# A convolution's shifted copies by quarters of the channels, chunk statistics moved behind the last step, and a layer norm in another order, in a two-layer trunk on one core

## The chip, the cores and the metric

One Trainium2 chip, one of its cores. The metric is device time of one launch in microseconds (us), median of three runs, beside the time of a second kernel. PE is TensorE's matmuls, PEld its weight loads, DVE is VectorE, ACT is ScalarE, POOL is GpSimd, SP is SyncE, which here issues nearly all transfers.

## The reference, cut to what matters

A latent sequence of 256 tokens and a context of 256 tokens (512 columns together), 1024 channels, two layers. Only the mixer of the first layer is touched:

```python
def conv_module(h, w1, b1, dw, dw_b, norm_g, w2):
    y = h @ w1 + b1
    a, gt = jnp.split(y, 2, axis=-1)
    y = a * jax.nn.sigmoid(gt)
    y = lax.conv_general_dilated(y, dw[:, None, :], window_strides=(1,),
        padding=[(15, 15)], dimension_numbers=('NWC', 'WIO', 'NWC'),
        feature_group_count=D_MODEL) + dw_b          # 31 taps, each channel by itself
    y = jax.nn.silu(layer_norm(y, norm_g))           # mean and variance over the 1024 channels
    return y @ w2
```

Beside it each layer needs `silu(c) @ ada_w` for both conditions, from which shift, scale and gate of every sub-layer come. Float32 products are made on TensorE from split operands: an operand is the sum of a high part and a low part, and one product is three matmuls (high by high, low by high, high by low; lines 201 to 203, `mm3`).

## The kernel before, in words

The 1024 channels are eight chunks of 128 partitions; a chunk has 512 columns. Step `s` of the loop over chunks makes the gate half `g` and the value half `a` of chunk `s` (each 24 matmuls of 128x128 by 512), multiplies them into `y`, and meanwhile convolves the chunks before it. Of the 31 taps of a chunk, 16 run on TensorE, the rest on DVE (`lacc`, L557 and L559) and on POOL with ACT (`pacc`, L537 to L546).

TensorE needs four shifted copies of `y` on four groups of 32 partitions. They come by way of DRAM: `bounce_out` (L505) writes `y` to a scratch `yd` of 4 quarters x 32 channels, `bounce_in` (L508 to L517) loads the diagonal weights `dg` and then the tile `z4` (its transfers show as `z<-yd`). `dwconv_pe` (L526, name `cv`) contracts over 32 channels x 4 shifts, a quarter of the channels at a time. Chunk `s`'s copies are asked for in step `s` and used in step `s + 2`. SP issues transfers strictly in the order written, and an issue that waits holds up those behind it. There are two `z4` tiles.

The order is written out by hand: `pin` keeps an instruction in program order on its engine. Around the steps stand twenty blocks of the adaptive weights (`ada` 0 to 19): `begin` is eight matmuls (L240), `evict` a copy on ACT (`adasb`), `cols` two matmuls with that copy (L252), `finish` two small ACT operations (`mods`). They fill TensorE where it would wait.

The layer norm's sums are taken per chunk by `stats` (L588): two matmuls with a 1/1024 weight, on the chunk and on its square (`square`, L583, ACT, two tiles). Chunks 0 to 3 are summed inside steps 6 and 7, ahead of the taps' matmuls; 4 to 7 after the last step. Then `srow` (ACT copy), `stats_t` (L771, sums to columns), `mean_bc` (L774, mean to all partitions), `mb` (ACT), eight subtractions on POOL (L790), the inverse root on DVE (L806 to L815), `rstd_bc` (L799), and for every chunk `zt` (DVE, L829), `zs` (ACT, Silu, L838), high part `ah_z` and low part `al_z` (DVE, L325 and L326). The product with `w2` (tiles `w`) follows, in two halves of 512 output channels; its weights come as `w2_00`, `w2_01` (first half), `w2_10`, `w2_11` (second half), each split into `wh` on ACT and `wl` on DVE. Three tiles hold raw weights.

Of the kernel before, what the change touches and what calls it, by code (L numbers as in the profile page):

```python
# [64 lines left out]
ADA_AUX = (16, 17, 18, 19)
ADA_K4 = (8, 9, 18)
# [17 lines left out]
def trunk_kernel(ctx: ExitStack, tc, x_in, ctx_in, cond, small, consts, rope, dist, ada, adas, adat,  # L84
# [67 lines left out]
    def load(src, n=2048, name="w", also=lambda i: None):  # L152
        raw = wp.tile([P, 2048], F32, tag="raw", name="raw_" + name)
        also(nc.sync.dma_start(raw[:, :n], src))
        return raw
# [333 lines left out]
    def glu(ch, pa, sg):  # L489
# [9 lines left out]
            pin(nc.gpsimd.tensor_tensor(yv, yv, sg, op=ALU.mult))  # L499
        return y  # L500

    def bounce_out(ch, y):

# [1 line left out]
        pin(nc.sync.dma_start(yd.rearrange("q c t -> (q c) t"), y.rearrange("p s t -> p (s t)")))  # L505
        return yd

    def bounce_in(ch, yd):  # L508

# [4 lines left out]
        w = 2 * YW - 3
        for s in range(4):
            pin(nc.sync.dma_start(z4[32 * s:32 * s + 32, :, 0:w], yd[:, :, s:s + w].rearrange("q c t -> c q t")))
# [64 lines left out]
    def square(ch):  # L581
        sqs[ch] = cv.tile([P, 512], F32, tag="sq", name="sq", bufs=2)
        pin(nc.scalar.activation(sqs[ch], yc[:, ch, :], AF.Square))  # L583

    def stats(ch):
        for i, src in enumerate((yc[:, ch, :], sqs.pop(ch))):
            q = 2 * (ch % 2) + i
            pin(nc.tensor.matmul(pst[32 * q:32 * q + 32, :], mean32, src, start=(ch < 2), stop=(ch >= KC - 2)))  # L588
# [143 lines left out]
    fills = [pA.tile([P, 4096], F32, tag=tag, name=f"raw_fill_{tag}") for tag in ("ah", "al")]
    pin(nc.gpsimd.memset(fills[0][:, 0:1], 0.0))
    for i in range(12, 16):
        t = fills[(i - 12) // 2][:, 2048 * (i % 2):2048 * (i % 2) + 2048]
# [3 lines left out]
    for i in (16, 17):
        t = cv.tile([P, 4, 2 * YW], F32, tag="z4", name=f"raw_ada{i}", bufs=Z4).rearrange("p q t -> p (q t)")[:, 0:2048]  # L740
        pin(nc.sync.dma_start(t, ada[ADA_PE.index(i)]))
        ada_raws[i] = halves(t)
# [17 lines left out]
    cols(11)  # L760
    total(d)
    finish(11)
    square(d)
    stats(KC - 1)
    begin(12)
# [2 lines left out]
    evict(12)
    ptk = aux("stats_t")
    for t in range(4):  # L770
        pin(nc.tensor.matmul(ptk[:, 2 * t:2 * t + 2], srow[:, P * t:P * t + P], sel2, start=True, stop=True))  # L771
    pmd = aux("mean_bc")
    for q in range(4):
        pin(nc.tensor.matmul(pmd[32 * q:32 * q + 32, :], sel2[:, 0:1].to_broadcast([P, 32]), srow, start=True, stop=True))  # L774
    mb = cv.tile([P, 512], F32, tag="sq", name="mb", bufs=2)
    begin(13)
    cols(12)
    pin(nc.scalar.activation(mb, pmd, AF.Copy))
    evict(13)
    finish(12)  # L780
    cols(13)
    finish(13)
    gate_to_rows(0, 0, pin)
    gates = [gate_bc(0, 0, 0, pin), gate_bc(0, 0, 1, pin)]
# [1 line left out]
    ada_raws[19] = ada_load(19, pin)
    begin(14)
    evict(14)
    for ch in range(KC):
        pin(nc.gpsimd.tensor_tensor(yc[:, ch, :], yc[:, ch, :], mb, op=ALU.subtract))  # L790
    st = cv.tile([P, 4, 2], F32, name="st")
    nc.vector.tensor_copy(st.rearrange("p t i -> p (t i)"), ptk[:, 0:8])
    md, vv = st[:, :, 0], st[:, :, 1]
# [12 lines left out]
    nc.vector.tensor_tensor(mq, md, md, op=ALU.mult)  # L806
# [4 lines left out]
    nc.vector.tensor_scalar(nh, va, -0.5, None, op0=ALU.mult)
    for i in range(3):
        nc.vector.tensor_tensor(pt, nh, rn, op=ALU.mult)
        nc.vector.tensor_tensor(pt, pt, rn, op=ALU.mult)
        nc.vector.scalar_tensor_tensor(rn, pt, 1.5, rn, op0=ALU.add, op1=ALU.mult)  # L815
# [1 line left out]
    cols(14)
    finish(14)
    begin(15)
    evict(15)  # L820
    cols(15)
    finish(15)
# [11 lines left out]
    for ch in range(KC):  # L834
        if ch + 1 < KC:
            z_norm(ch + 1)
        zs = pz[ch % 2]
        pin(nc.scalar.activation(zs, zts[ch], AF.Silu, scale=cn[:, ch:ch + 1]))  # L838
        split_to(z[0][:, ch, :], z[1][:, ch, :], zs, pin)
        if ch == W2_AT:  # L840
            split_w2(0, 1, None, pin)
        if ch in (2, 4):
            begin(15 + ch // 2)
            evict(15 + ch // 2)
        if ch in (3, 5):
            cols(15 + ch // 2)
            finish(15 + ch // 2)
    cvs.close()
    pB = ctx.enter_context(tc.tile_pool(name="pB", bufs=1))
    for i in range(2):  # L850
# [28 lines left out]
        for _ in range(min(n, len(adr))):  # L879
            ada_next(adr.pop(0))  # L880

    for n in range(2):
# [4 lines left out]
        w = kview(w2p[n, 0] + w2p[n, 1], 512)
        order = ([(t, k) for k in range(KC) for t in range(4)] if n == 0
                 else [(t, k) for t in range(4) for k in range(KC)])
        for t, k in order:  # L890
# [5 lines left out]
            if not n and t == 3 and k in (3, 5):  # L896
                begin(18 + k // 5)
                evict(18 + k // 5)
            if not n and t == 3 and k in (4, 6):
                cols(18 + k // 6)  # L900
                finish(18 + k // 6)
# [568 lines left out]
```

## Time and profile before

| | |
|---|---|
| runs | 1097.85 us median, 1096.79 to 1098.8 |
| profiled execution | 1100.03 us, its span 1098.2 us |
| PE busy over the span | 1069.6 us (97%) |
| steps with the taps, 60.00 to 154.86 us | PE busy 92.41 of 94.86 us |
| last value half to first matmul with `w2`, 154.86 to 185.52 us | PE busy 27.04 of 30.66 us |
| from there to the next norm's first transposes, 185.52 to 232.01 us | PE busy 46.49 of 46.49 us |
| median landing of one `z<-yd` transfer of 284.5 KB | 5.2 us |

The span runs from the first to the last instruction; the execution's own time is 1.8 us more. In rows of a timeline or of the chain of waits the first number is the start, the second the duration. In rows of stretches each engine has its busy time and its instructions, and at the end stand TensorE's granted clock, the share of the 16 DMA engines, and GB/s.

### The profile page before, as it was taken

Reading aid. Unit: us, or ns where it says so; the run is one execution under the profiler, and the core shown is the slowest. Engines: PE = TensorE matmul, PEld = TensorE weight load, DVE = VectorE, ACT = ScalarE, POOL = GpSimd, SP = SyncE. Lnnn points to the kernel's source line nnn. Section 1 sums busy time; section 2 is a strip of 40 time slices with the busy share of each in tenths; the row PEclk is TensorE's granted clock in tenths of the full one; section 3 lists DMA queues with packets and bytes.
Section 4 is the critical chain, followed back from the end, with each engine's and each line's share of the span. In section 5 each row is a group of like instructions: output and inputs, shape, how many; then the busy total and the mean of one; then the engine's idle time right before and its main releaser. Section 6 shows DMA issues by size and latency. Waiting matters only on the chain.

```text
span 1098.2 us, 13530 instructions
## 1 busy us (share of the span) xinstructions
PE 1069.6 (97%) x5322; PEld 844.4 (77%) x5322; DVE 696.1 (63%) x1138; ACT 418.6 (38%) x610; POOL 161.7 (15%) x120
## 2 busy tenths in 40 slices
PE   7899998999999999999999999999999989999998
PEld 4566655788888888888888788888888868888886
DVE  4797874667999886636554786357454555555445
ACT  5473564344221222212231663324332453444442
POOL 0076863030000000000000430000000461000000
PEclk9999999999999999999999999999999999999999
DMA  9477778822576677433323342234233344455551
GB/s 367 183 191 224 221 211 330 346 94 81 203 252 230 230 272 255 163 115 115 115 75 118 139 157 93 111 134 163 106 115 115 115 159 159 167 186 192 192 182 49
DMA packets 35185, 190.16 MB, mean 173 GB/s; under 512 B 3953, under 2 KB 4657, under 8 KB 16049
## 3 DMA queue, kind: packets, MB, share of 16 engines
q1 hardware_dynamic: 34688, 188.01, 48.9%
q10 hardware_dynamic: 434, 1.29, 0.3%
q8 instruction: 42, 0.69, 0.3%
q14 instruction: 21, 0.17, 0.0%
HBM read 185.86 MB, written 3.42 MB: 172 GB/s over the span
## 4 chain that ended last, share of the span: by engine, by line
PE 88%; DVE 4%; ACT 3%; DMA 2%; issue 1%; POOL 1%; SPq 0%; ACTq 0%; POOLq 0%
PE u L203 4%; PE u L201 4%; PE fa L202 4%; PE u L202 4%; PE fa L203 4%; PE fb L202 4%; PE fa L201 4%; PE fb L203 4%; PE fb L201 4%; PE v L202 3%; PE v L203 3%; PE v L201 3%; PE dn L203 3%; PE dn L201 3%; PE dn L202 3%; PE g L201 2%
## 5 line engine op out<-in xcount | busy, mean ns | idle before, releaser
L172 DVE TENSOR_TENSOR wl_gu<-raw_gu,wh_gu 128x1024 fp32r<-128x1024 f32 x76 | 92.2, 1222 | 82.3 <-ACT wh_gu L164 81.5
L164 ACT ACTIVATE wh_gu<-raw_gu 128x1024 fp32r<-128x1024 f32 x84 | 88.0, 1058 | 139.3 <-PE fb L202 52.6
L870 DVE SCALAR_TENSOR_TENSOR junk<-raw_adat,crow 128x1024 f32<-128x1024 f32 x80 | 97.7, 1221 | 0.9
L172 DVE TENSOR_TENSOR wl_dn<-raw_dn,wh_dn 128x1024 fp32r<-128x1024 f32 x38 | 46.5, 1224 | 45.5 <-ACT wh_dn L164 45.2
L201 PE MATMUL fa<-ah_h0f,wh_gu 128*128 128x512 f32 (+1 forms) x192 | 72.0, 376 | 1.0 <-DVE ah_h0f L325 1.0
L202 PE MATMUL fa<-al_h0f,wh_gu 128*128 128x512 f32 (+1 forms) x192 | 72.2, 376 | 0.1
L201 PE MATMUL fb<-ah_h0f,wh_gu 128*128 128x512 f32 (+1 forms) x192 | 72.1, 376 | 0.0
L203 PE MATMUL fa<-ah_h0f,wl_gu 128*128 128x512 f32 (+1 forms) x192 | 72.0, 375 | 0.0
L202 PE MATMUL fb<-al_h0f,wh_gu 128*128 128x512 f32 (+1 forms) x192 | 72.0, 375 | 0.0
L203 PE MATMUL fb<-ah_h0f,wl_gu 128*128 128x512 f32 (+1 forms) x192 | 72.0, 375 | 0.0
L164 ACT ACTIVATE wh_dn<-raw_dn 128x1024 fp32r<-128x1024 f32 x38 | 40.3, 1060 | 80.3 <-PE dn L203 35.5
L201 PE MATMUL u<-wh_gu,ah_h1f 128*128 128x512 f32 x160 | 63.6, 397 | 0.0
L172 POOL TENSOR_TENSOR wl_qk<-raw_qk,wh_qk 128x1024 fp32r<-128x1024 f32 x4 | 9.6, 2397 | 362.6 <-DVE res L356 350.1
L202 PE MATMUL u<-wl_gu,ah_h1f 128*128 128x512 f32 x160 | 62.5, 392 | 0.0
L203 PE MATMUL u<-wh_gu,al_h1f 128*128 128x512 f32 x160 | 62.4, 391 | 0.0
L542 POOL TENSOR_TENSOR pacc<-pacc,pr 128x512 f32<-128x512 f32 x39 | 58.7, 1506 | 17.9 <-ACT pr L541 15.6
L559 DVE SCALAR_TENSOR_TENSOR lacc<-y,sm,lacc 128x512 f32<-128x512 f32 x65 | 49.1, 755 | 2.1
L202 PE MATMUL v<-wl_v,ah_h 128*128 128x512 f32 x128 | 50.4, 393 | 0.0
L203 PE MATMUL v<-wh_v,al_h 128*128 128x512 f32 x128 | 50.1, 391 | 0.0
L201 PE MATMUL dn<-wh_dn,ah_hid 128*128 128x512 f32 x128 | 49.9, 390 | 0.0
L202 PE MATMUL dn<-wl_dn,ah_hid 128*128 128x512 f32 x128 | 49.8, 389 | 0.0
L203 PE MATMUL dn<-wh_dn,al_hid 128*128 128x512 f32 x128 | 49.8, 389 | 0.0
(309 smaller groups left out, 2665.2 us busy)
## 6 DMA issues: line engine op xcount, KB each, us to landing
raw_gu<-in_gu_dram SPq DMA_DIRECT2D x44, 1024.0 KB, 4.8
raw_adat<-in_adat_dram SPq DMA_DIRECT2D x28, 1024.0 KB, 4.8
raw_dn<-in_dn_dram SPq DMA_DIRECT2D x19, 1024.0 KB, 4.7
raw_ada<-in_ada_dram SPq DMA_DIRECT2D x11, 1024.0 KB, 11.0
z<-yd SPq DMA_DIRECT2D x32, 284.5 KB, 5.2
raw_qk<-in_wqk_dram SPq DMA_DIRECT2D x8, 1024.0 KB, 4.7
raw_v<-in_wv_dram SPq DMA_DIRECT2D x8, 1024.0 KB, 4.8
raw_g<-in_wg_dram SPq DMA_DIRECT2D x8, 1024.0 KB, 4.8
```

Source lines behind the costliest of these rows:

```text
L164: also(nc.scalar.activation(hi[:, :m], raw[:, c:c + m], AF.Copy))
L172: also((eng or nc.vector).tensor_tensor(lo[:, :m], raw[:, c:c + m], hi[:, :m].bitcast(F32), op=ALU.subtract))
L201: also(nc.tensor.matmul(o, a[0], b[0], start=first, stop=False))
L202: also(nc.tensor.matmul(o, a[0], b[1], start=False, stop=False))
L203: also(nc.tensor.matmul(o, a[1], b[0], start=False, stop=last))
L542: pin(nc.gpsimd.tensor_tensor(pacc, pacc, pr, op=ALU.add))
L559: pin(nc.vector.scalar_tensor_tensor(cacc, a, w, cacc, op0=ALU.mult, op1=ALU.add))
L870: pin(nc.vector.scalar_tensor_tensor(junk, raw[:, c, :], 1.0, crow[:, s, :], op0=ALU.mult, op1=ALU.mult, accum_out=mods[l][:, c0 + c, s:s ...
```

## The change

- The four transfers that fill `z4` go by quarter of the channels and no longer by shift: each writes 128 partitions (32 channels x 4 shifts) of one quarter's columns, instead of 32 partitions (one shift) of all quarters. Bytes and number of transfers stay. Partitions are now ordered channel by shift, and the weights `dwd` are laid out to match.
- `dg` is asked for in `bounce_out`, ahead of `y`'s way out.
- Chunks 0 to 5 are squared and summed after the last step, between the blocks 8 to 11, chunk 6 after them. Chunk 7 has sums of its own: eight matmuls with one column straight into `stats_t`, added on DVE. The mean goes out by `token_row`, as the inverse root does.
- The inverse root stands ahead of block 13, most of its operands in PSUM.
- `ah_z` is written by a second ACT operation with Silu; DVE's cast is gone.
- Blocks 13 to 19 stand later, four of them within the first half of the `w2` product; the gates' transfers stand behind the load of `w2_10`. Blocks 14, 15 and 19 load into `z4` tiles, 12 and 13 into one freed tile instead of two, and 16 into small tiles.

```diff
@@ bounce_out, bounce_in
+        n = GROUPS[ch]
+        dgs[ch] = cv.tile([P, MAXG, 4, 32], F32, tag="dg", name="dg", bufs=2)
+        pin(nc.sync.dma_start(dgs[ch][:, :n], dwd[:, ch, :n]))
         yd = dr.tile([4, 32, 2 * YW], F32, name=f"yd{ch}")
...
-        for s in range(4):
-            pin(nc.sync.dma_start(z4[32 * s:32 * s + 32, :, 0:w], yd[:, :, s:s + w].rearrange("q c t -> c q t")))
-        return z4, dg
+        for q in range(4):
+            src = yd[q]
+            pin(nc.sync.dma_start(z4[:, q, 0:w], bass.AP(src.tensor, src.offset, [[2 * YW, 32], [1, 4], [1, w]])))
+        return z4, dgs.pop(ch)
@@ inside the steps
-        if step >= KC - 2:
-            stats(2 * (step - KC + 2))
-            stats(2 * (step - KC + 2) + 1)
...
-        if step >= KC - 3:
-            i = 2 * (step - KC + 3)
-            square(i)
-            square(i + 1)
+        if step == KC - 1:
+            square(0)
+            square(1)
@@ after the last step
     cols(8)
     finish(8)
     begin(9)
-    stats(4)
-    stats(5)
-    square(c)
+    stats(0)
+    stats(1)
+    square(2)
+    square(3)
     evict(9)
     begin(10)
     cols(9)
     finish(9)
+    stats(2)
+    stats(3)
+    square(4)
+    square(5)
     evict(10)
...
+    for i, src in enumerate((yc[:, d, :], sqs.pop(d))):
+        for t in range(4):
+            pin(nc.tensor.matmul(ptk[:, 16 + 2 * t + i:17 + 2 * t + i], src[:, P * t:P * t + P], mean32[:, 0:1],
+                                 start=True, stop=True))
+        if not i:
+            begin(12)
+    pin(nc.vector.tensor_tensor(st[:, 1, :], ptk[:, 16:24], st[:, 0, :], op=ALU.add))
...
+    pmd = token_row(md, "mean_bc")
@@ for every chunk of z
+        pin(nc.scalar.activation(z[0][:, ch, :], zts[ch], AF.Silu, scale=cn[:, ch:ch + 1]))
         pin(nc.scalar.activation(zs, zts[ch], AF.Silu, scale=cn[:, ch:ch + 1]))
-        split_to(z[0][:, ch, :], z[1][:, ch, :], zs, pin)
+        pin(nc.vector.tensor_tensor(z[1][:, ch, :], zs, z[0][:, ch, :].bitcast(F32), op=ALU.subtract))
         if ch == W2_AT:
             split_w2(0, 1, None, pin)
+        if ch == 0:
+            finish(13)
+            evict(14)
+            load_to(19, z4_tile(19))
+            w2r[1, 0] = load(w2[1, 0], name="w2_10", also=pin)
+        if ch == 1:
+            cols(14)
+            finish(14)
+            gate_to_rows(0, 0, pin)
+            gates = [gate_bc(0, 0, 0, pin), gate_bc(0, 0, 1, pin)]
...
+    w2r[1, 1] = load(w2[1, 1], name="w2_11", also=pin)
@@ first half of the w2 product
+        if t == 3 and k in W2_ADA:
+            i = 17 + W2_ADA.index(k)
+            if i > 17:
+                cols(i - 1)
+                finish(i - 1)
+            if i < 20:
+                begin(i)
+                evict(i)
```

The first place is SP's queue around chunk 1's copies (`yd1` is chunk 1 in DRAM). Before:

```order
L505 DMA yd1_586<-y_579 128x572 [waits DMAHW3_49,Pool_49]
L512 DMA dg_588<-in_dwd_dram 128x512
L516 DMA z4_590<-yd1_586 32x4x569 [waits DMAHW5_49,DMAHW3_49]
L516 DMA z4_590<-yd1_586 32x4x569 [waits DMAHW6_49]
L154 DMA raw_w1b5_698<-in_w1b_dram 128x2048 [waits DMAHW1_49,DVE_49]
```

The same place in the change:

```order
L509 DMA dg_586<-in_dwd_dram 128x512 [waits DMAHW3_49]
L511 DMA yd1_588<-y_579 128x572 [waits DMAHW4_49,Pool_49]
L520 DMA z4_590<-yd1_588 128x1x569 [waits DMAHW4_49]
L520 DMA z4_590<-yd1_588 128x1x569 [waits DMAHW6_49]
L155 DMA raw_w1b5_698<-in_w1b_dram 128x2048 [waits DMAHW1_49,DVE_49]
```

`dg` moved ahead of `yd1`, and each copy writes 128 partitions.

The second place is TensorE from the taps of the last chunk (`cv7`) to `rstd_bc`. Before:

```order
L526 MATMUL cv7_1490<-z4_1365,dg_1363 32x512 x15
L252 MATMUL ada11_1481<-cst_81,adasb_1507 128x2 [waits Activation_49]
L588 MATMUL stats_529<-yc_528,cst_81 32x512 [waits DVE_49]
L588 MATMUL stats_529<-sq_1515,cst_81 32x512 [waits Activation_49]
L240 MATMUL ada12_1519<-raw_fill_ah_1426,csil_113 32x256 x7
L771 MATMUL stats_t_1532<-cst_81,srow_1528 128x2 [waits Activation_49]
L774 MATMUL mean_bc_1537<-srow_1528,cst_81 32x512 [waits PE_49]
L240 MATMUL ada13_1543<-raw_fill_ah_1426,csil_113 32x256 x7
L252 MATMUL ada13_1543<-cst_81,adasb_1555 128x2 [waits Activation_49]
L287 MATMUL gr00_1563<-cst_81,gcs_1564 16x128 [waits PE_49,Activation_49]
L240 MATMUL ada14_1581<-raw_fill_al_1427,csil_113 32x256 x7
L799 MATMUL rstd_bc_1618<-cst_81,rn_1604 128x128 [waits DVE_49]
```

The same place in the change:

```order
L530 MATMUL cv7_1492<-z4_1349,dg_1345 32x512 x12
L792 MATMUL stats_t_1523<-cst_81,srow_1486 128x2 [waits Activation_49]
L797 MATMUL stats_t_1523<-cst_81,yc_528 128x1 [waits DVE_49]
L241 MATMUL ada12_1534<-raw_fill_1410,csil_113 32x256 x7
L797 MATMUL stats_t_1523<-cst_81,sq_1521 128x1 [waits Activation_49]
L785 MATMUL mean_bc_1551<-cst_81,st_1528 128x128 [waits DVE_49]
L241 MATMUL ada13_1580<-raw_fill_1410,csil_113 32x256 x7
L253 MATMUL ada12_1534<-cst_81,adasb_1549 128x2 [waits Activation_49]
L785 MATMUL rstd_bc_1593<-cst_81,rn_1566 128x128 [waits DVE_49,Activation_49]
```

The sums of chunks 0 to 6 stand ahead of `cv7` now, and one block less stands between `cv7` and `rstd_bc`.

The third place is ACT within the first half of the `w2` product, from the value of chunk 5 on. Before:

```order
L838 ACTIVATE zs1_1645<-zt_1691,sm_79 128x512 [waits DVE_49]
L259 ACTIVATE mods0_107<-ada17_1696,sm_79 128x2 [waits PE_49]
L838 ACTIVATE zs0_1644<-zt_1707,sm_79 128x512 [waits DVE_49]
L838 ACTIVATE zs1_1645<-zt_1716,sm_79 128x512 [waits DVE_49]
L164 ACTIVATE wh_w2_10_1883<-raw_w2_10_1728 128x1024 [waits DMAHW4_49]
```

The same place in the change:

```order
L845 ACTIVATE ah_z_1611<-zt_1684,sm_79 128x512 [waits DVE_49]
L846 ACTIVATE zs1_1614<-zt_1684,sm_79 128x512
L165 ACTIVATE wh_w2_10_1889<-raw_w2_10_1628 128x1024 [waits DMAHW1_49]
L260 ACTIVATE mods0_107<-ada16_1689,sm_79 128x2 [waits PE_49]
L845 ACTIVATE ah_z_1611<-zt_1700,sm_79 128x512 [waits DVE_49]
```

The split of `w2_10`, which waits for its load, moved ahead of the values of chunks 6 and 7.

More of the change, by code (lines that the diff above doesn't have):

```diff
@@ L63 @@
 W2_AT = 3
+W2_ADA = (3, 4, 5, 6)
 PACC = 2
[L65 to L66 removed]
+ADA_AUX = (14, 15, 16, 17, 18, 19)
+ADA_K4 = (8, 9, 16)
 T2 = 5
@@ L587, in stats @@
             q = 2 * (ch % 2) + i
-            pin(nc.tensor.matmul(pst[32 * q:32 * q + 32, :], mean32, src, start=(ch < 2), stop=(ch >= KC - 2)))
+            pin(nc.tensor.matmul(pst[32 * q:32 * q + 32, :], mean32, src, start=(ch < 2), stop=(ch >= KC - 3)))
     ys, zs4, cbs = {}, {}, {}
@@ L730, in trunk_kernel, with load_to, z4_tile @@
     dve_taps(d, cut, TAPS)
[L732 to L735, printed above, removed]
+    def load_to(i, t):
         pin(nc.sync.dma_start(t, ada[ADA_PE.index(i)]))
         ada_raws[i] = halves(t)
+    def z4_tile(i):
+        return cv.tile([P, 4, 2 * YW], F32, tag="z4", name=f"raw_ada{i}", bufs=Z4).rearrange("p q t -> p (q t)")[:, 0:2048]
+    fill = pA.tile([P, 4096], F32, tag="ah", name="raw_fill")
+    for i in (12, 13):
+        load_to(i, fill[:, 2048 * (i % 2):2048 * (i % 2) + 2048])
+    load_to(14, z4_tile(14))
     w2r[0, 1] = load(w2[0, 1], name="w2_01", also=pin)
[L739 to L742, printed above, removed]
     cols(8)
@@ L752, in trunk_kernel @@
     finish(9)
+    stats(2)
+    stats(3)
+    square(4)
+    square(5)
     evict(10)
-    stats(c)
+    begin(11)
     cols(10)
     finish(10)
-    begin(11)
-    cbs[d] = dwconv_pe(d, zs4.pop(d))
+    stats(4)
+    stats(5)
+    square(c)
     evict(11)
[L760 to L765, printed above, removed]
+    stats(c)
     srow = t2("srow")
     pin(nc.scalar.activation(srow, pst, AF.Copy))
[L768 to L784, printed above, removed]
-    ada_raws[18] = ada_load(18, pin)
[L786 to L793, printed above, removed]
+    cols(11)
+    finish(11)
+    cbs[d] = dwconv_pe(d, zs4.pop(d))
+    load_to(15, z4_tile(15))
+    ada_raws[16] = ada_load(16, pin)
+    ada_raws[17] = ada_load(17, pin)
+    ada_raws[18] = ada_load(18, pin)
+    total(d)
+    square(d)
     def token_row(cols, name):
@@ L816, in trunk_kernel @@
-    prs = token_row(rn, "rstd_bc")
[L817 to L822, printed above, removed]
+    ptk = aux("stats_t")
+    for t in range(4):
+        pin(nc.tensor.matmul(ptk[:, 2 * t:2 * t + 2], srow[:, P * t:P * t + P], sel2, start=True, stop=True))
+    st = cv.tile([P, 2, 8], F32, name="st")
+    pin(nc.vector.tensor_copy(st[:, 0, :], ptk[:, 0:8]))
+    for i, src in enumerate((yc[:, d, :], sqs.pop(d))):
+        for t in range(4):
+            pin(nc.tensor.matmul(ptk[:, 16 + 2 * t + i:17 + 2 * t + i], src[:, P * t:P * t + P], mean32[:, 0:1],
+                                 start=True, stop=True))
+        if not i:
+            begin(12)
@@ new lines, in trunk_kernel @@
+    pin(nc.vector.tensor_tensor(st[:, 1, :], ptk[:, 16:24], st[:, 0, :], op=ALU.add))
+    pin(nc.vector.tensor_tensor(ptk[:, 24:32], ptk[:, 16:24], st[:, 0, :], op=ALU.add))
+    md, vv = (st[:, 1, :].rearrange("p (t i) -> p t i", i=2)[:, :, i] for i in range(2))
+    mdp = ptk[:, 24:32].rearrange("p (t i) -> p t i", i=2)[:, :, 0]
+    evict(12)
+    pmd = token_row(md, "mean_bc")
+    mb = cv.tile([P, 512], F32, tag="sq", name="mb", bufs=2)
+    pin(nc.scalar.activation(mb, pmd, AF.Copy))
+    for ch in range(KC):
+        pin(nc.gpsimd.tensor_tensor(yc[:, ch, :], yc[:, ch, :], mb, op=ALU.subtract))
@@ new lines, in trunk_kernel @@
+    rn = cv.tile([P, 4], F32, name="rn")
+    mq, va, nh, pt = (ptk[:, c:c + 4] for c in (32, 36, 8, 12))
+    pin(nc.vector.tensor_tensor(mq, mdp, md, op=ALU.mult))
+    pin(nc.vector.scalar_tensor_tensor(va, vv, EPS, mq, op0=ALU.add, op1=ALU.subtract))
+    pin(nc.vector.tensor_scalar(rn.bitcast(I32), va.bitcast(I32), -0.5, 1597463007.0, op0=ALU.mult, op1=ALU.add))
+    pin(nc.vector.tensor_scalar(nh, va, -0.5, None, op0=ALU.mult))
+    for i in range(3):
+        pin(nc.vector.tensor_tensor(pt, nh, rn, op=ALU.mult))
+        pin(nc.vector.tensor_tensor(pt, pt, rn, op=ALU.mult))
+        pin(nc.vector.scalar_tensor_tensor(rn, pt, 1.5, rn, op0=ALU.add, op1=ALU.mult))
@@ L824, in trunk_kernel @@
+    begin(13)
+    cols(12)
+    evict(13)
+    prs = token_row(rn, "rstd_bc")
+    cols(13)
+    finish(12)
+    begin(14)
     z = new_act(pA, "z")
@@ L837, in trunk_kernel, with w2_order @@
         zs = pz[ch % 2]
+        pin(nc.scalar.activation(z[0][:, ch, :], zts[ch], AF.Silu, scale=cn[:, ch:ch + 1]))
         pin(nc.scalar.activation(zs, zts[ch], AF.Silu, scale=cn[:, ch:ch + 1]))
-        split_to(z[0][:, ch, :], z[1][:, ch, :], zs, pin)
+        pin(nc.vector.tensor_tensor(z[1][:, ch, :], zs, z[0][:, ch, :].bitcast(F32), op=ALU.subtract))
         if ch == W2_AT:
             split_w2(0, 1, None, pin)
+        if ch == 0:
[8 more added lines that the diff above has]
+            gates = [gate_bc(0, 0, 0, pin), gate_bc(0, 0, 1, pin)]
         if ch in (2, 4):
-            begin(15 + ch // 2)
-            evict(15 + ch // 2)
+            begin(14 + ch // 2)
+            evict(14 + ch // 2)
         if ch in (3, 5):
-            cols(15 + ch // 2)
-            finish(15 + ch // 2)
+            cols(14 + ch // 2)
+            finish(14 + ch // 2)
+    w2r[1, 1] = load(w2[1, 1], name="w2_11", also=pin)
+    def w2_order(n):
+        return ([(t, k) for k in range(KC) for t in range(4)] if n == 0
+                else [(t, k) for t in range(4) for k in range(KC)])
+    pw = [acc(f"w2_0{t}") for t in range(4)]
+    w = kview(w2p[0, 0] + w2p[0, 1], 512)
+    for t, k in w2_order(0):
+        tk = slice(P * t, P * t + P)
+        mm3(pw[t], (z[0][:, k, tk], z[1][:, k, tk]), w(k), k == 0, k == KC - 1)
+        if k == KC - 1:
+            residual(t, 0, pw[t], gates[t // 2])
+        if t == 3 and k in W2_ADA:
[6 more added lines that the diff above has]
+                evict(i)
     cvs.close()
     pB = ctx.enter_context(tc.tile_pool(name="pB", bufs=1))
-    for i in range(2):
-        w2r[1, i] = load(w2[1, i], name=f"w2_1{i}", also=pin)
     ads = ExitStack()
@@ L880, in fill_rows @@
             ada_next(adr.pop(0))
-    for n in range(2):
+    for n in (1,):
         pw = [acc(f"w2_{n}{t}") for t in range(4)]
-        if n:
-            split_w2(n, 0)
-            split_w2(n, 1)
+        split_w2(n, 0)
+        split_w2(n, 1)
         w = kview(w2p[n, 0] + w2p[n, 1], 512)
-        order = ([(t, k) for k in range(KC) for t in range(4)] if n == 0
-                 else [(t, k) for t in range(4) for k in range(KC)])
-        for t, k in order:
+        for t, k in w2_order(n):
             tk = slice(P * t, P * t + P)
@@ L895, in trunk_kernel @@
                 residual(t, n, pw[t], gates[t // 2], last)
[L896 to L901, printed above, removed]
             if n and (t, k) == (1, KC - 1):
```

18 lines of the change are left out of this document (3 added, 15 removed).

## The prediction

> **What bounds the kernel now.** I read the page's busy times first, then the stretches around the changed code, then TensorE's own waits, and last the transfers behind the longest wait.
>
> ```profile
> PE 1069.6 (97%) x5322; PEld 844.4 (77%) x5322; DVE 696.1 (63%) x1138; ACT 418.6 (38%) x610; POOL 161.7 (15%) x120
> ...
> 60.00:154.86 94.86, 92.41 (x498) 60.52 (x497) 76.74 (x87) 51.56 (x75) 69.85 (x56) 0.98 0.80 227
> 154.86:185.52 30.66, 27.04 (x282) 13.47 (x282) 15.46 (x33) 13.23 (x37) 15.03 (x13) 1.00 0.84 297
> 185.52:232.01 46.49, 46.49 (x244) 36.66 (x245) 33.17 (x59) 17.74 (x31) 1.29 (x2) 1.00 0.64 249
> ```
>
> TensorE is busy 97% of the span, so a change is worth what it takes from TensorE's idle time, from its slow stretches and from its list of work. In the changed code it idles 94.86 - 92.41 = 2.45 us during the steps and 30.66 - 27.04 = 3.62 us between the last step and the first `w2` matmul, and not at all after that. Who it waits for between 60 and 235 us:
>
> ```profile
> PE cv L526 <- DMA z<-yd: 3.5, 2, 2.3
> PE w L201 <- DVE ah_z L325: 0.8, 1, 0.8
> PE ada L252 <- ACT adasb L246: 0.7, 2, 0.6
> ```
>
> The longest single wait, 2.3 us, is for a chunk's shifted copies. The chain of waits places it, and shows a second cost:
>
> ```profile
> 75.59 6.87 DMA z<-yd
> 82.55 5.34 PE cv L526 x32
> ...
> 99.94 3.57 PE cv L526 x32
> ...
> 129.29 1.00 PE stats L588 x8
> ...
> 144.83 1.00 PE stats L588 x8
> ```
>
> Chunk 1's taps start at 82.55, and the same 32 matmul records that take 3.57 us in the next chunk take 5.34. The clock says why:
>
> ```profile
> 82.00:83.00 1.00, 0.45 (x5) 0.20 (x9) 0.96 (x2) 0.38 (x2) 0.92 (x2) 1.00 1.03 426
> 83.00:84.00 1.00, 1.00 (x16) 0.46 (x12) 1.00 (x2) 1.00 (x2) 1.00 (x1) 0.92 0.93 358
> 84.00:85.00 1.00, 1.00 (x12) 0.36 (x7) 1.00 (x1) 0.16 (x1) 0.92 (x2) 0.50 0.61 230
> ...
> 87.00:88.00 1.00, 1.00 (x9) 0.18 (x2) 1.00 (x2) 0.00 (x0) 1.00 (x1) 0.87 1.00 303
> ```
>
> Right behind the wait the granted clock falls to 0.50 until about 87.3. So this wait costs 2.30 + (5.34 - 3.57) = 4.07 us.
>
> Why are the copies late? Compare the DMA columns (busy share, GB/s) while four such copies move with those while loads of 128 partitions move:
>
> ```profile
> 161.00:165.00 4.00, 3.85 (x40) 1.86 (x36) 3.86 (x6) 1.65 (x6) 3.11 (x4) 1.00 1.03 209
> 167.00:171.00 4.00, 3.91 (x35) 1.46 (x36) 0.21 (x1) 0.00 (x0) 0.00 (x0) 1.00 1.01 422
> ```
>
> The engines are fully busy in both, yet the copies get 209 GB/s and the loads 422.
>
> **The copies by quarters.** Four copies of 284.5 KB are 1.165 MB: 1.165 / 209 = 5.6 us before. The new form has not run, so I bound its rate by the two rows: 209 GB/s if the many reads of the same rows set it, 422 (2.8 us) if the 32 partitions do. I take 422, because every copy now reaches the partitions that the fast loads reach. [...]
>
> ```profile
> 62.90 1.75 SPq L516 DMA_DIRECT2D z<-yd  x4
> 64.75 0.38 SPq L154 DMA_DIRECT2D raw_w1b<-in_w1b_dram  x1
> 70.31 0.34 SPq L505 DMA_DIRECT2D yd<-y  x1
> 73.82 2.20 SPq L516 DMA_DIRECT2D z<-yd  x4
> ...
> 156.01 0.34 SPq L505 DMA_DIRECT2D yd<-y  x1
> 158.76 2.57 SPq L516 DMA_DIRECT2D z<-yd  x4
> ```
>
> For chunk 1 the saving counts twice: chunk 0's copies and a 1 MB load are ahead of `yd1` in the engines, so `yd1` lands sooner too. By the copies alone, what lands at 75.59 + 6.87 = 82.46 lands 2.8 us earlier, 79.7, when TensorE is still in the gate half of chunk 3 until 82.55 - 2.30 = 80.25. `yd1` sooner is a reserve of some 0.9 us (73.82 - 70.31 = 3.5 us to land, against 158.76 - 156.01 = 2.75 for chunk 7's). `dg` ahead of it costs no wait: its tile is free, and on SP `yd1` is held up only by `y` itself; in the engines its 256 KB take about 0.6 us at 422 GB/s, less than that reserve. In later steps `dg` also waits for TensorE's taps two chunks before, which end ahead of `y`. Value: the whole 4.07 us; if only 209 holds, nothing.
>
> Does the rest keep pace 4 us earlier? DVE is the tightest. In the chain of its work the next wait is:
>
> ```profile
> 96.97 0.75 DVE L557 TENSOR_SCALAR lacc<-y,sm 128x512 f32<-128x512 f32 x1 [5.06 <-POOL y L499]
> 95.75 1.19 POOL L499 TENSOR_TENSOR y<-y,sg 128x512 f32<-128x512 f32 x1 [7.12 <-ACT y L498]
> ```
>
> DVE stood idle 5.06 us and POOL 7.12 before chunk 3's `y`, which follows TensorE. Both give up 4 of them and still wait for TensorE.
>
> **Statistics out of the steps.** Two groups of 1.00 us leave steps 6 and 7 (start to start 0.88 each): -1.76 there. They come back in the next stretch, where I count them.
>
> **From the last step to `w2`.** I laid the new order of TensorE out with durations from the chain of waits, taps 3.55 us and two chunks of sums 0.88 (above), a block of `ada` 0.86 and `cols` 0.54:
>
> ```profile
> 174.20 0.98 PE stats_t L771 x8
> 175.19 0.99 PE mean_bc L774 x8
> 176.18 0.86 PE ada L240 x16
> 177.04 0.54 PE ada L252 x4
> ...
> 180.10 1.09 PE rstd_bc L799 x8
> ```
>
> Counted from the end of the last value half: blocks 8 to 11 with `cols` (4 x 1.40), chunk 6's taps (3.55) and seven chunks of sums (3.1) are 12.3 us. The new squares stand on ACT ahead of `adasb`:
>
> ```profile
> L583 ACT ACTIVATE sq<-yc 128x512 f32<-128x512 f32 x8 | 4.8, 623 | 4.1 <-DVE yc L649 2.6 <-PE stats L588 1.5
> L246 ACT ACTIVATE adasb<-ada 128x256 f32<-128x256 f32 x12 | 4.5, 377 | 7.2 <-PE ada L240 7.2
> ```
>
> With two square tiles, a pair of squares (2 x 0.62) and `adasb` (0.38) start when the sums before them end, and TensorE has one block (0.86) to fill with, so with the handovers it waits 0.8 to 0.9 us, twice, and 0.7 for chunk 6's square: 2.4. Taps of chunk 7 thus end at 12.3 + 2.4 + 3.55 = 18.25. Its copies wait for nothing by then: before, they landed at 160.90 + 6.06 = 166.96, 12.1 us after the last value half, so the old wait here (3.5 - 2.3 = 1.2 us) goes whatever the rate. Then `stats_t` and its two new groups (each four matmuls that load 128 columns, priced like the 0.98 row; bounds 0.5 to 1.1), one block, and DVE's sum, for which it waits 0.4: the mean starts at 18.25 + 0.98 x 3 + 0.86 + 0.4 = 22.5. On DVE the chain of the inverse root was:
>
> ```profile
> 175.42 0.16 DVE L806 TENSOR_TENSOR mq<-st 128x4 f32<-128x4 f32 x1
> 177.71 0.16 DVE L815 SCALAR_TENSOR_TENSOR rn<-stats_t,rn 128x4 f32<-128x4 f32 x1
> ...
> 181.30 1.28 DVE L829 TENSOR_TENSOR zt<-yc,rstd_bc 128x512 f32<-128x512 f32 x2 [3.43 <-PE rstd_bc L799]
> ```
>
> Thirteen operations in 2.45 us; now one more, 2.7, so `rstd_bc` starts at 25.2. From there `zt` comes 1.2 us later (180.10 to 181.30), takes 0.64 (1.28 for two), Silu 0.69, and with two handovers of 0.15 `w2` starts at 28.05 instead of 30.66: -2.6.
>
> **The `w2` stretch.** Before, it held three blocks and four `cols` beside 180 matmuls. Now it holds five and six, and `gr` (0.35). A piece with nothing but matmuls gives their price:
>
> ```profile
> 192.49:195.21 2.72, 2.72 (x13) 2.25 (x12) 2.72 (x4) 0.00 (x0) 0.00 (x0) 1.00 1.04 429
> ```
>
> 2.72 / 12 = 0.227. So 46.49 = 180 x 0.227 + 5.6, that is 1.1 per block and 0.58 per `cols`, and the new stretch takes 50.2: +3.7. Per chunk TensorE needs twelve of them, 2.7 us, ACT now two Silu operations and DVE two of much the same length:
>
> ```profile
> L838 ACT ACTIVATE zs<-zt,sm 128x512 f32<-128x512 f32 x8 | 5.4, 691 | 2.5 <-DVE zt L829 2.5
> ```
>
> 1.4 us each, hidden under TensorE's 2.7. POOL's subtractions, of the size of its 1.19 us for `y`, keep ahead of that too. The weights' splits on ACT I come to under the rivals; I take their waits as nothing.
>
> **Sum.** -4.07 - 1.76 - 2.6 + 3.7 = -4.7 us. Nothing after 232 us is in another order. Span 1098.2 to 1093.5, profiled execution 1100.03 to 1095.3, median 1097.85 to 1093.1 (it stood 2.2 below the profiled execution).
>
> **The rivals.** (a) The copies are no faster. For it: no row shows rows of a scratch read four times by one engine. Against it: 209 with engines fully busy. Then chunk 1 gives nothing, the rest -0.7: 1097.2.
>
> (b) Half of chunk 1's gain stays away. Either DVE, with 5.06 - 4.07 = 1.0 us left, becomes late, or the slow clock has another cause than the wait. [...] What speaks for the wait as cause is that the clock is still 1.00 during the wait and falls right behind it, while shorter waits (1.2 us before chunk 7's taps, in a stretch at 1.00) leave it alone. If the dip stays, -4.7 + 1.8 gives 1095.0.
>
> (c) Slower: ACT stands on `w2_10`. Its split now stands on ACT ahead of `ah_z` of chunks 6 and 7, and its load is issued only after DVE has split `w2_01`, by my order 12 us into the `w2` stretch; TensorE wants `ah_z` of chunk 6 at 21.7.
>
> ```profile
> DMA to landing us min/median/max: 9.1/12.0/14.0
> ...
> raw_gu<-in_gu_dram SPq DMA_DIRECT2D x44, 1024.0 KB, 4.8
> ```
>
> If it lands as a lone load does (4.8, last row) ACT is through at 20; 1.6 us to spare. If it takes the 12.0 of the four `raw_w` loads before (first row), ACT gives `ah_z` at 27.4, 5.7 late; `w2_11`, which waits for the same tile, is as late again: -4.7 + 11 = 1104; at 9.1, 2.8 + 2.5 late, 1098.5. It decides from about 11 us of landing on. Against it: those loads were queued behind others of the same kind, and here the queue is empty by then.
>
> (d) More: waits of ACT (2.4) fall away or the new sums take 0.5 instead of 0.98 a group: up to -7.5, 1090.4.
>
> **How the numbers follow.** My forecast 0.68, its own range 1091.2 to 1095.2 (new sums 1 us to the good, 2 us of waits more). (a) 0.10, (b) 0.09, (c) 0.07, (d) 0.06. The range for 8 in 10 reaches from the middle of (d) over (a): 1090.8 to 1097.8. A measurement tells from no change what exceeds 0.2%, 2.2 us, so faster means under 1095.65: nearly all of the forecast and (d), most of (b): 0.78. Same: (a), some of (b) and of the forecast's edge: 0.15. Slower: (c) 0.07.
>
> **What would show it.** `z<-yd` lands in some 3.5 us instead of 5.2, near 400 GB/s while four move. Taps of chunk 1 start within 0.5 us of the matmuls before, take about 3.6 us, and the clock stays at 1.00 there. Last value half to first `w2` matmul 28 us, the rest to the transposes 50. Wrong, if the wait for copies stays above 1 us, if the clock still falls near 80 us, or if TensorE waits for ACT's `ah_z` or `wh_w` by more than 2 us.

## The result, and the profile after

The changed kernel takes 1101.45 us (median; 1097.28 to 1107.27), the kernel before 1097.97 in the same comparison: a ratio of 1.003 with a 95% interval of 1.0019 to 1.0042. It became slower by 3.5 us; I had said 4.7 us faster. The profiled execution took 1102.06 us, its span is 1100.3.

The stretches of the changed kernel, from 60 us on cut at the same events as before (columns as in the prediction): steps up to the last value half, from there to the first `w2` matmul, from there to the first transposes, the rest.

```profile
60.00:152.23 92.23, 90.88 (x482) 59.36 (x481) 77.03 (x87) 50.24 (x72) 70.74 (x57) 1.00 0.67 234
152.23:184.17 31.94, 29.79 (x269) 15.90 (x268) 15.03 (x34) 12.66 (x31) 10.88 (x9) 0.89 0.82 309
184.17:234.25 50.08, 50.08 (x287) 38.70 (x288) 28.33 (x52) 25.30 (x50) 5.61 (x6) 1.00 0.54 198
234.25:1100.00 865.75, 853.65 (x4019) 703.03 (x4017) 535.09 (x875) 304.13 (x404) 73.13 (x34) 1.00 0.43 154
```

Against before: the last value half ends 2.6 us sooner (152.2 for 154.86; forecast 5.8), the way to `w2` takes 31.9 us for 30.66 (forecast 28.05), `w2` takes 50.1 for 46.5 (forecast 50.2), the rest is unchanged. Two things stand out: the steps gave back less than half of what was expected, and in the second row the clock column reads 0.89.

TensorE's waits between 60 and 240 us:

```profile
PE ada L253 <- ACT adasb L247: 1.4, 2, 0.7
PE cv L530 <- DMA z<-yd: 1.3, 1, 1.3
...
PE w L202 <- ACT ah_z L845: 0.3, 1, 0.3
PE stats_t L797 <- DVE st L794: 0.3, 1, 0.3
PE mean_bc L785 <- DVE st L802: 0.3, 1, 0.3
```

The wait for chunk 1's copies is still there. Its length (1.3) understates it, since TensorE now waits quarter by quarter and part of the waiting stands with the weight loads (2.26 us ahead of the one at 83.41). The timeline shows what chunks 0 and 1 cost, where 32 records of taps alone take 3.57:

```profile
70.56 4.48 PE L530 MATMUL cv<-z,dg 128*32 128x512 f32 x32
...
80.63 1.44 PE L530 MATMUL cv<-z,dg 128*32 128x512 f32 x6
83.41 3.62 PE L530 MATMUL cv<-z,dg 128*32 128x512 f32 x26 [1.35 <-DMA z<-yd]
86.97 0.50 PE L202 MATMUL a<-ah_h,wh_w1b 128*128 128x512 f32 x1
```

Chunk 0 takes 4.48 (0.9 too long), chunk 1 takes 86.97 - 80.63 = 6.34 (2.8 too long): 3.7 us lost, against 4.07 before. The chain of waits shows what is late (start, duration):

```profile
62.86 0.59 POOL pacc L546
...
64.24 1.29 POOL pacc L546
65.61 2.17 POOL pacc L546
67.84 2.16 POOL pacc L546
70.00 1.15 POOL y L500
71.17 4.12 DMA yd<-y
...
77.17 6.20 DMA z<-yd
83.41 3.62 PE cv L530 x26
```

`y` of chunk 1 is made only after POOL's four sums for chunk 0, `yd1` lands 4.12 us after its issue (3.5 before), and the last of the four copies 6.20 after its own (6.87 before).

The clock in the second stretch, in rows that I cut where it changes:

```profile
167.60:171.06 3.46, 3.46 (x34) 1.05 (x34) 0.00 (x0) 0.66 (x3) 0.00 (x0) 1.00 0.99 419
171.06:174.47 3.41, 3.15 (x36) 2.35 (x32) 0.85 (x2) 0.63 (x1) 0.00 (x0) 1.00 0.77 264
174.47:181.30 6.83, 6.57 (x39) 4.76 (x36) 2.33 (x15) 1.36 (x3) 1.62 (x2) 0.50 1.01 380
160.82:164.23 3.41, 2.68 (x32) 1.41 (x31) 2.33 (x4) 1.83 (x5) 0.79 (x1) 1.00 0.92 326
```

From 174.47 to 181.30 TensorE ran at half clock. In the 3.41 us ahead of that it was *busy* for 3.15, so it hardly idled; for two thirds of that time it ran, by the chain of waits, matmuls with one or two columns (`stats_t`), and for the rest the end of the taps (0.3 us) and most of a block (0.8):

```profile
171.38 1.00 PE stats_t L792 x8
172.62 1.05 PE stats_t L797 x8
173.67 1.10 PE ada L241 x16
174.77 1.81 PE stats_t L797 x8
176.83 2.08 PE mean_bc L785 x8
178.91 1.86 PE ada L241 x16
180.77 0.80 PE ada L253 x4
181.57 1.01 PE rstd_bc L785 x8
```

Behind 174.47 the second new group takes 1.81 for 1.05, the mean 2.08 for 1.0, the block 1.86 for 1.0, and `rstd_bc` follows the mean's start by 4.74 us where DVE's chain needs 2.7. That is 0.76 + 2.04 = 2.8 us.

### The profile page after: what moved, and what is told of

The parts are those of the page before. It is cut to its first block, busy times and chain, and to the rows that moved or that the text cites. A ratio compares the mean times of both kernels' runs of the same rounds, so it can differ in the third digit from the quotient of the medians.

```text
span 1100.3 us, 13555 instructions
## 1 busy us (share of the span) xinstructions
PE 1074.9 (98%) x5334; PEld 848.2 (77%) x5334; DVE 691.7 (63%) x1132; ACT 423.1 (38%) x618; POOL 161.8 (15%) x119
## 4 chain that ended last, share of the span: by engine, by line
PE 90%; DVE 4%; ACT 2%; DMA 2%; issue 1%; POOL 1%; SPq 0%; ACTq 0%; POOLq 0%; DVEq 0%
PE u L204 4%; PE u L202 4%; PE u L203 4%; PE fa L203 4%; PE fa L204 4%; PE fb L203 4%; PE fb L204 4%; PE fa L202 4%; PE fb L202 4%; PE v L203 3%; PE v L204 3%; PE v L202 3%; PE dn L203 3%; PE dn L204 3%; PE dn L202 3%; PE cv L530 2%
## 5 line engine op out<-in xcount | busy, mean ns | idle before, releaser
L173 DVE TENSOR_TENSOR wl_dn<-raw_dn,wh_dn 128x1024 fp32r<-128x1024 f32 x38 | 46.5, 1225 | 45.4 <-ACT wh_dn L165 45.1
L204 PE MATMUL v<-wh_v,al_h 128*128 128x512 f32 x128 | 50.1, 391 | 0.0
```

What stands on the lines that cost most here:

```text
L173: also((eng or nc.vector).tensor_tensor(lo[:, :m], raw[:, c:c + m], hi[:, :m].bitcast(F32), op=ALU.subtract))
L204: also(nc.tensor.matmul(o, a[1], b[0], start=False, stop=last))
```

## The experiments

Two theories came from these lines. **S**: chunk 1 is late because of *when* its `y` is made, and the new copies are hardly quicker than the old; its rival: the copies did bring 4 us and the rest ate them. **N**: matmuls of few columns don't hold the clock up, and the two new groups of sums make a stretch of them long enough to halve it; its rival: idle time halved it. All ratios are to the kernel before, with 95% intervals.

| kernel | median us | ratio |
|---|---|---|
| copies_only | 1097.32 | 0.9995 (0.9983 to 1.0008) |
| tail_only | 1101.5 | 1.0025 (1.0016 to 1.0035) |
| y1_early | 1097.88 | 1.0000 (0.9988 to 1.0011) |
| wide | 1099.36 | 1.0008 (0.9998 to 1.0019) |
| narrow | 1100.16 | 1.003 (1.0014 to 1.0046) |
| stats_first | 1099.47 | 1.0014 (1.0000 to 1.0028) |
| y1_before | 1102.38 | 1.0041 (1.0026 to 1.0057) |
| y1_copies | 1095.16 | 0.9969 (0.9957 to 0.9982) |
| y1_wide | 1097.19 | 0.9990 (0.9981 to 1.0000) |

### The change in two halves

`copies_only` is the kernel before with these two pieces of the change (`dg` ahead of `yd`, and the copies by quarters, with `dwd` laid out to match), `tail_only` the change without them:

```diff
+        dgs[ch] = cv.tile([P, MAXG, 4, 32], F32, tag="dg", name="dg", bufs=2)
+        pin(nc.sync.dma_start(dgs[ch][:, :n], dwd[:, ch, :n]))
-        for s in range(4):
-            pin(nc.sync.dma_start(z4[32 * s:32 * s + 32, :, 0:w], ...))
+        for q in range(4):
+            pin(nc.sync.dma_start(z4[:, q, 0:w], ...))
```

> The kernel before with the new copies (by quarters, the rows of dg issued ahead of yd) and nothing else of the change. Theory S (the time at which chunk 1's y is ready decides, and the new copies reach only about 290 GB/s): TensorE still waits for chunk 1's copies by 1 us or more, and the time is that of the kernel before, ratio 0.998 to 1.001. Rival R (the copies are worth the 4 us of the prediction, and the rest of the change ate them): 1094, ratio 0.9963.

> The change without its copies: shifted copies and dg as before, statistics, layer norm and ada blocks as changed. Theory T (the new tail costs time, by a clock at half behind the narrow sums): about 1101, ratio 1.002 to 1.004, with a granted clock of 0.50 somewhere between the last taps and the first w2 matmul. Rival (the tail is worth the 0.7 us of the prediction and the loss comes from the copies): 1097.3, ratio 0.9994.

The copies alone change nothing that can be measured, and the tail alone brings nearly the whole loss. TensorE's wait in `copies_only`, and the clock in `tail_only` between chunk 7's taps and `w2`:

```profile
PE cv L529 <- DMA z<-yd: 1.5, 1, 1.5
```

```profile
172.00:178.60 6.60, 6.34 (x44) 4.20 (x36) 2.33 (x15) 0.98 (x2) 0.78 (x1) 0.50 0.97 364
```

So the rival of S falls (it wanted 1094 for the copies alone), and the slow clock belongs to the tail: it is there with the old copies too.

`tail_only` shows something else. It has the old copies, and `y` of chunk 1 at its old time, yet its wait is 1.36 us for 2.30, and the taps behind it run at full clock (3.64 for 5.34):

```profile
81.23 3.64 PE L527 MATMUL cv<-z,dg 128*32 128x512 f32 x32 [1.36 <-DMA z<-yd]
```

So the 4.07 us of the prediction are what the wait cost in one execution; in this one the same copies cost 1.4. The new copies differ as much: the profiled executions of `narrow`, `wide`, `stats_first` and the changed kernel, all alike up to there, lose 1.7, 2.3, 3.5 and 3.6 us by chunks 0 and 1 (from the start of chunk 0's taps to that of chunk 2's, less the 24.81 that it takes in `y1_early`, where TensorE waits for no copies).

### Does the time of y decide?

`y1_early` is the changed kernel with chunk 1's gate product, and its way out, ahead of chunk 0's taps on ACT and POOL:

```diff
+        if step == 1:
+            pa, pg = pa0[step]
+            sg = glu_gate(step, pg)
+            ys[step] = glu(step, pa, sg)
+            yd1 = bounce_out(step, ys[step])
+            zs4[0] = bounce_in(0, yd0)
         if d >= 0:
             pool_taps(d)
...
+            elif step == 1:
+                zs4[1] = bounce_in(1, yd1)
+                w1_load(step + W1_AHEAD)
```

> The changed kernel with chunk 1's gate product ahead of chunk 0's six taps on ACT and POOL, its way out ahead of chunk 0's copies, and the 1 MB load of w1b behind chunk 1's copies. Theory S: yd1 is issued some 8 us sooner, TensorE waits for no copies of chunk 1, its 32 records take 3.6 us, and the time is 2 to 4 us less than the changed kernel's, ratio to the kernel before 0.9995 to 1.001. Rival Q (the copies' rate in the queue decides): TensorE waits as long as before, now for chunk 0 or 1, and the time is that of the changed kernel, ratio 1.003.

3.6 us less than the changed kernel, as theory S had it, and about the 3.7 us that chunks 0 and 1 had lost. In the chain of waits both now take their plain 3.57:

```profile
71.70 3.57 PE cv L530 x32
80.93 3.57 PE cv L530 x32
```

Then the same move in the kernel before, without and with the new copies:

> The kernel before, nothing of the change, with chunk 1's gate product, its way out and its copies early as in y1_early. Theory S (the issue time of yd1 decides): no wait for chunk 1's copies and no slow clock behind it; in the trace of before that is 4.07 us, in a run with the wait but without the slow clock 1.4 to 2.3: 1094 to 1096.5, ratio 0.9965 to 0.9987. Rival Q (the rate in the queue decides): as before, ratio 1.000.

> The kernel before with the new copies by quarters and chunk 1 early, without the new tail. Theory S: as y1_before, and the wait for chunk 7's copies in the tail (1.2 us of the kernel before) goes too: 1093 to 1095.5, ratio 0.9955 to 0.998. If the new copies are worth nothing anywhere: the same time as y1_before.

Here theory S, as I had put it, failed. `y1_before` is *slower* by 0.4%, while `y1_copies` is the fastest of all kernels that compute the same result, 0.3% under the kernel before. The landing times of the eight copies of chunks 0 and 1 say why; the first row is `y1_before`'s wait, the second its landings (least, median, most):

```profile
PE cv L526 <- DMA z<-yd: 5.9, 2, 4.9
```

```profile
DMA to landing us min/median/max: 6.2/10.6/11.3
```

and `y1_copies`:

```profile
DMA to landing us min/median/max: 4.1/5.3/5.6
```

With two chunks' copies in flight at once the old form takes twice as long, and chunk 0's come late in place of chunk 1's (a wait of 4.9 us; behind it the clock is at half for 3.4 us, and the taps take 5.29). The new form carries both, and TensorE waits for neither. So the time of `y` and the form of the copies decide together: as tried here, each alone brings nothing or harm, both bring 2.7 us. That fits `copies_only`, which shows no gain: with a single chunk in flight, the flow is not what binds. An early `y` is not the only cure, though: in `own_rows` below the wait for chunk 1 goes without it.

### How fast are the new copies?

Chunk 6's copies have the queue nearly to themselves. The changed kernel over five microseconds of their flow (last columns: DMA share, GB/s), and the landing times of these four:

```profile
145.00:150.00 5.00, 5.00 (x31) 3.12 (x24) 3.19 (x5) 4.59 (x7) 4.05 (x4) 1.00 0.89 280
```

```profile
DMA to landing us min/median/max: 3.2/3.5/4.6
```

The kernel before, the same two views:

```profile
147.00:152.00 5.00, 5.00 (x36) 2.80 (x29) 2.60 (x4) 2.41 (x4) 3.84 (x3) 1.00 1.01 219
```

```profile
DMA to landing us min/median/max: 3.6/4.6/5.5
```

280 GB/s, not the 422 that I took, for a set of four by itself; each copy lands about 1 us sooner in the median, but even the quickest of them takes 3.2 us (3.6 before). Moreover, SP needs longer to issue four of them: 2.46 us in the changed kernel (start of the first to end of the last) against 1.75 in the kernel before (for chunk 1, 2.46 against 2.20). Two more kernels asked what holds the rate down, each with the source of the copies changed in `copies_only` (the first new line is `no_shift`, the second `own_rows`); both leave out the shifts, so their result is another:

```diff
-    bass.AP(src.tensor, src.offset, [[2 * YW, 32], [1, 4], [1, w]])
+    bass.AP(src.tensor, src.offset, [[2 * YW, 32], [0, 4], [1, w]])
+    yd.rearrange("q c t -> (q c) t")[:, 0:w]
```

> A look at the copies' rate: copies_only with all four rows of a group read at offset 0, so the taps are computed from unshifted rows; bytes, packets, partitions and repeated reads stay. In the changed kernel four copies with nothing else in the queue moved 280 GB/s. If the odd start of the rows holds the rate down: 340 GB/s or more there (chunk 6). If not: 270 to 300.

> A look at the copies' rate: copies_only with each copy reading 128 rows once, unshifted, instead of 32 rows four times, so the taps are computed from other rows; bytes, packets and partitions stay. If reading the same rows four times holds the rate down: 340 GB/s or more for chunk 6. If it is the size of the packets (2.3 KB a row) or the queue: 270 to 300, as no_shift.

`no_shift`: 273 to 317 GB/s in the full microseconds of chunk 6's flow, so the odd start of the rows is not it. `own_rows`, over four microseconds of chunk 6's, and the issue of chunk 1's copies:

```profile
142.00:146.00 4.00, 4.00 (x40) 1.10 (x30) 0.60 (x2) 1.82 (x3) 3.77 (x4) 1.00 0.83 267
```

```profile
73.32 1.75 SPq L519 DMA_DIRECT2D z<-yd  x4
```

No higher rate over these four either, below the bound that I had set for the repeated reads. It is weak evidence: SP took 2.42 us to issue these four, and single microseconds among them reach 355 GB/s. But SP issues chunk 1's four in 1.75 us again, everything behind them on SP moves up (`yd1` lands 2.4 us after its issue, for 4.1 in `copies_only`), and TensorE waits for no copies of chunk 1; the time is 1094.87 us. Both kernels ran once only.

The trace of `y1_copies` says more. In this microsecond the second of two sets is in flight, and by the size of the packets (2,276 bytes, a row of a copy) all that moves is copies:

```profile
73.00:74.00 1.00, 1.00 (x13) 0.35 (x16) 0.96 (x3) 0.37 (x2) 1.00 (x2) 1.00 1.03 385
```

So neither the size of the rows nor their repeated reading holds the new form at 280: behind another set it comes near the 422 that I took. For chunk 6, a packet of a copy takes 0.09 us in the changed kernel and 0.18 in the kernel before (medians). What keeps a set by itself below that rate was not tried.

### What halves the clock?

`wide` adds six matmuls of 512 columns whose result nobody reads, two behind `stats_t` (L792) and two behind each of the two new groups (L797); `narrow` is the same with 2 columns:

```diff
+    def wide(n):
+        for i in range(n):
+            m = w2p[0, 0][0][0]
+            pin(nc.tensor.matmul(pst, m[:, 0:128], m[:, 0:512], start=True, stop=True))
...
+    wide(2)
```

> The changed kernel with six more matmuls of 512 columns, whose result nobody reads, two behind each of the narrow groups L792, L797, L797: 6 x 0.23 = 1.4 us more work for TensorE. Theory N (a clock window with hardly anything but narrow matmuls halves the clock): the clock is at half for less time between the last taps and the first w2 matmul, often not at all, and the time falls by about 2 us against the changed kernel, ratio to the kernel before about 1.001. Rival I (TensorE's idle waits halve it): the dip stays and the time rises by 0.8 to 1.4 us, ratio 1.004.

> The kernel of wide with its six extra matmuls at the same places, each of 2 columns instead of 512. Theory N (it is the columns that flow, not the instructions, that keep the clock up): the clock falls to half there as in the changed kernel, and the time is the changed kernel's plus 0.3 to 0.6 us, ratio 1.003 to 1.004. Rival I (any instruction in the gaps keeps it up): the clock stays at 1.00 and the time falls by 2 to 2.5 us, ratio 1.001.

More work made the kernel faster than the changed kernel by 2.1 us (the two intervals just touch). The chain of waits of `wide`:

```profile
170.29 0.98 PE stats_t L797 x8
171.27 0.57 PE stats L793 x2
...
173.63 0.67 PE stats L793 x2
...
175.08 0.59 PE stats L793 x2
175.71 1.16 PE mean_bc L785 x8
176.87 1.00 PE ada L241 x16
178.41 1.01 PE rstd_bc L785 x8
```

The clock is 1.00 throughout, the mean takes 1.16 and the block 1.00, and `rstd_bc` follows the mean's start by 2.70, DVE's own time. In `narrow`, the 3.41 us ahead of the drop, and the slow stretch behind it:

```profile
169.10:172.51 3.41, 3.37 (x38) 2.58 (x34) 0.86 (x2) 0.63 (x1) 0.00 (x0) 1.00 0.76 247
172.50:179.50 7.00, 6.94 (x42) 5.30 (x39) 2.33 (x15) 1.13 (x3) 1.31 (x2) 0.51 0.97 378
```

TensorE is busy for 3.37 of 3.41 us, and then at half clock for 6.8. Hardly any idle time is left, and as many instructions were added as in `wide`; only the columns are missing. (Its time tells less: the median is 1.3 us under the changed kernel's, where I had expected 0.3 to 0.6 over it, and the intervals overlap.) With the row at 160.82 of the changed kernel (busy 2.68 of 3.41 us, clock 1.00 after it) this rules out idle time as the cause of this drop, and theory N stands. The mean granted clock of all executions agrees: its median is 0.9965 for `wide` (0.995 to 0.999), 0.994 for `narrow` (0.990 to 0.996) and 0.993 for the changed kernel (0.989 to 0.997).

`stats_first` puts the first narrow group ahead of chunk 7's taps and block 12 right behind them; the work is the same.

> The changed kernel with the first narrow group (stats_t of seven chunks) ahead of chunk 7's taps, and the ada block 12 right behind the taps instead of between the two new groups. The same work in another order. Theory N: 1.3 us less of narrow work stand together, the clock is at half for less time on average, and a wait of 0.3 goes: 0.5 to 2.5 us less than the changed kernel, ratio to the kernel before 1.001 to 1.0025. If the order doesn't matter to the clock: ratio 1.003.

2.0 us less than the changed kernel by the medians; in its trace the clock is at half for 3.4 us instead of 6.8. The two intervals overlap, so the gain is likely rather than shown.

Its trace also says what to count. This stretch has hardly more than four matmuls of 512 columns, one after the other, and the clock stays at 1.00 behind it:

```profile
165.37:168.78 3.41, 3.26 (x20) 1.52 (x14) 0.00 (x0) 1.85 (x5) 0.00 (x0) 1.00 1.02 430
```

About 2,000 columns flow in it, against some 4,600 in the stretch ahead of the changed kernel's drop, most of them four matmuls at a time (in taps and blocks four records start within 0.02 us). The time tells them apart, not the number: matmuls of 128 or more columns run here for 1.88 us, there for 1.19. I cut all thirteen traces, from 60 to 1085 us, into pieces of 3.41 us whose edges fall on the changes of the clock. The 23 pieces followed by half clock have such matmuls for 0 to 1.50 us, the other 3,878 for 1.64 us or more. Idle time and narrow matmuls count alike there: the piece ahead of the kernel before's drop at 83.84 has 1.30 us of taps, and the rest is the wait for chunk 1. (Ahead of 60 us this does not hold without exception: three pieces with 1.7 to 2.0 us, and two with 3.1, are followed by half clock too.)

> The changed kernel with both: chunk 1 early (y1_early) and the six wide matmuls (wide). If the two losses are separate, the savings of 3.6 and 2.1 us add: 1095.8, ratio to the kernel before 0.998. If one cure takes what the other took: 1097.5 or more, ratio 0.9995 or more.

`y1_wide` lands between the two forecasts: the cures together save 4.3 us, 1.4 less than their sum. In the trace of `y1_early` the slow stretch had already been 3.4 us long instead of 6.8, so `wide` had less to cure there. The mean clock of `y1_early`'s twelve executions (median 0.995, for 0.993 in the changed kernel) suggests that this was no accident of one execution; why the move shortens the slow stretch stays open.

## Why the prediction was wrong, point by point

**The copies by quarters (-4.07): wrong; with the way to `w2` one of two failures of much the same size.** The step that failed is "I take 422, because every copy now reaches the partitions that the fast loads reach". A set by itself runs at 280 GB/s, and I had priced it as bytes over rate only: a copy lands no sooner than 3.4 us after its issue in the kernel before and 3.0 in the changed one, SP takes up to 0.7 us longer to issue four, and `dg` ahead of `yd1`, which I had called free, is still in the queue (it lands 8.1 us after its issue) when `yd1` needs 4.12 us for 3.5. For a single set the row nearest to the truth was 209, and rival (a), copies that are worth nothing, is what `copies_only` shows; that its 1097.2 us lies by 1097.32 is chance, since it has the 0.7 of the rest in it. One sign of being right did come, the landing (forecast 3.5 us), as did the clock of 1.00 at chunk 1:

```profile
z<-yd SPq DMA_DIRECT2D x32, 284.5 KB, 3.6
```

But TensorE needs the last copy of chunk 1, and that one took 6.20. The saving itself was priced too high: 1.77 of the 4.07 is a slow clock that neither `tail_only` nor `copies_only` has at chunk 1. In the rows at chunk 6 the old form moves 219 GB/s with the engines full and the new one 280; the second of two sets of the new form reaches 385. That four copies by themselves would run at the 422 of the loads, and that (a) was worth only 0.10, was my estimate; no trace had shown such copies, and it failed. I also followed the landing back only to `yd1`; the four sums of POOL ahead of `y`, which the chain of waits of before shows as well, I did not weigh.

**Statistics out of the steps (-1.76): right.** In the chains of the two traces, the taps of chunks 3, 4 and 5 start 14.67 us apart in the changed kernel; with the groups in place (`copies_only`) 15.67 and 15.54: 1.9 us.

**From the last value half to `w2` (28.05): wrong, for want of the clock.** It took 31.9 us, 3.9 over the forecast, and 2.8 of that is the slow clock worked out above. The step that failed is the price of the new groups and of what follows them, "priced like the 0.98 row": that row ran at full clock, and these halve it. None of my rivals had it: I looked for the clock only at waits. The other 1.1 is small sizes. In `wide`, which holds the clock, the stretch is 29.86 us, of which its six matmuls take 0.57 + 0.67 + 0.59 = 1.83: without them 28.0, as forecast; but there they also cover two waits of 0.3, and the new groups run in 0.79 instead of 1.05. Two more sizes were off and cancelled: the waits for `adasb` were 1.4 us where I counted 2.4 with chunk 6's square, but that square comes so late that the chunk's two sums run one after the other.

**The `w2` stretch (50.2): right**, 50.1, with five blocks in it (15 to 19), as the sum counts them, and not the four of the list of changes.

**The rivals.** (c), ACT standing on `w2_10`, did not come: TensorE waits for `ah_z` 0.3 us and for no `wh_w`. (b) named the clock, but at chunk 1. Of the slower outcome, to which I gave 0.07, I had the sign and the price (up to 1104), and the wrong mechanism.

**Sum by the steps** (profiled executions): steps -2.6 instead of -5.8, way to `w2` +1.3 instead of -2.6, `w2` +3.6 instead of +3.7, together +2.3; the spans differ by +2.1. The medians differ by 3.5: the changed kernel's executions range over 10 us, those of before over 4.4, and in the changed kernel's the mean granted clock goes with the time, from 0.997 (1097.28 us) to 0.990 (1107.27).

## What to carry to other kernels

When a transfer is late, follow it back past its issue to whatever makes its data, and past its rate to its fixed time and to the queue in front of it; a faster form pays only where the flow is what binds, and it may show its worth only together with an earlier start. A loss read from one execution can be a third as large in the next: here the wait for chunk 1 cost 4.1 us in one trace and 1.4 in another, with the same copies. When TensorE's path is filled with matmuls of one or two columns, busy time is no measure of whether the clock holds: add up the time that wide matmuls run in each 3.4 us (in these traces, from 60 to 1085 us, 1.64 us or more kept the clock, 1.50 or less did not), put a block with many columns between narrow groups, and read the granted clock in rows as short as that. A term that moves work from one place to another (here 1.76 us out, 3.7 in) is worth only what idle time it fills.
